# A decoder layer on one core: the residual's factor folded into its addition, an early table load, two banks and one transpose given later ticks

## The chip, the cores and the metric

The kernel runs on one core of one Trainium2 chip. A core has five engines that work side by side, each through its own queue of instructions in program order: TensorE (PE) multiplies matrices out of SBUF into PSUM, VectorE (DVE) and ScalarE (ACT) do elementwise work, GpSimd (POOL) does some too, and SyncE (SP) issues most of the DMA transfers. An instruction that waits holds everything behind it in its own queue. The metric is the time of one execution in microseconds (us) on the device; less is better.

## The reference

One decoder layer on a prompt of 512 tokens and on 8 samples of one token each. What matters here, cut down:

```
x (512 x 1024 prompt rows, 8 x 1024 sample rows), ALPHA = 2 ** 0.25
h   = x * (1 + scale) + shift                    # adaLN from c @ w_ada
att = block-sparse attention, 8 heads of 64      # samples: over a paged K/V cache
mls = matrix memory (mLSTM), 4 heads of 128      # samples: from the states C, n, m
mix = concat(att, mls) @ w_out
x1  = layernorm(ALPHA * x + gate1 * mix)         # first residual
f   = (silu(h2 @ w_gate) * (h2 @ w_up)) @ w_down # h2: x1 modulated
y   = layernorm(ALPHA * x1 + gate2 * f)          # second residual
```

The outputs are y, the new K/V rows and the updated mLSTM states, all fp32.

## The kernel before

Each fp32 matrix is split into a high and a low part (`whi`, `wlo`; `hT_hi`, `hT_lo`; `mixM_hi`, `mixM_lo`; `h_hi`, `h_lo`), and a product is three matmuls. The weights come in 512 KB tiles (`raw`) by DMA, are cast on ACT (`whi`, L240) and subtracted on DVE (`wlo`, L241), and are then used by the main matmuls (L406 in the projections and the FFN's start, L665 in the FFN's body).

The whole program is one list, written in the order of recording. Main matmuls run in groups of six, and after each group a `tick()` lets every side job ("lane") record its next piece, then records the split of one weight tile, then issues loads. `yield n` in a lane means: come back n ticks later. So a lane's `yield` decides between which main groups its instructions stand in each engine's queue. PSUM has 8 banks of 512 columns, handed out in a queue: the bank given back first is taken next, and its new user waits until the last reader of the old contents is done. `put_later` gives a bank back one tick after the recording of that reader, `banks.put` at once:

```
    def put_later(*bs):

        def later():
            banks.put(*bs)
            return
            yield
        spawn(later(), 1)
```

The places that the change touches, in the order of time:

- Samples' attention (L1318 to L1327): the probabilities are transposed on PE into the bank `ps_sp` (L1321, L1322), copied out by DVE (L1325, L1326, written to `vo` by the trace's names), and the bank is given back. Some groups later `ps_pv` (L1339, L1342, L1352) takes the products with the values, DVE masks them (`Z`, L1356), and that bank is given back.
- Samples' mLSTM (L1544 to L1553): ACT scales the heads' rows (L1544), DVE multiplies them by the gate (L1547), PE transposes them (L1551, `ps_h`), and DVE copies the result (`mixsT`, L1553). Around it in time lies the end of the prompt's mLSTM: the keys' scaling (ACT L1196, `mk`), the heads' outputs (ACT L1122, `hm`; PE L1140, `ps_hm`; ACT L1145 and DVE L1146 to `mixM_hi` and `mixM_lo`), and the new states (PE L1205, `ps_C`; ACT L1208).
- `ln1_rows` (L1590 on) loads the prompt's rows x1 and multiplies the four tiles by ALPHA on ACT (L1597), one a tick; then, among other things, it loads the samples' rows `xs` (L1603) and computes the columns of the first norm.
- `residual` (L1636) computes `rtmp = ps * gate` (L1639) and `dst = dst + rtmp` (L1640). The out-projection's `ev_out` calls it eight times, for four row tiles by two halves; the samples' rows and the second residual call it too.
- `ln_rows` (L1618) loads the norm's vectors lg and lb (L1623, L1624) and, 12 ticks after their loads, multiplies them by ALPHA on ACT (L1628).
- The FFN's start, `ffn_first`, with the first Silu at L1821; `ln1_tile` (L1707, L1711, L412) prepares its rows tile by tile.

Of the kernel before, what the change touches and what calls it, by code (L numbers as in the profile page):

```python
# [13 lines left out]
AF = mybir.ActivationFunctionType  # L14
ALU = mybir.AluOpType
AX = mybir.AxisListType.X

P = 128
# [3 lines left out]
NT = 4  # L22
# [8 lines left out]
ALPHA = 2.0 ** 0.25  # L31
# [15 lines left out]
def decoder_layer(  # L47
# [7 lines left out]
    nc = tc.nc  # L55
# [34 lines left out]
    banks = Slots(pp, "b", 8, 512)  # L90
# [18 lines left out]
    TT = nc.vector.tensor_tensor  # L109
    TS = nc.vector.tensor_scalar  # L110
    STT = nc.vector.scalar_tensor_tensor
    VCOPY = nc.vector.tensor_copy
    ACOPY = nc.scalar.copy
    ACT = nc.scalar.activation
    PT_ = nc.gpsimd.tensor_tensor
# [14 lines left out]
    def spawn(gen, delay=0):  # L130
        lanes.append([clock[0] + delay, gen])
# [25 lines left out]
# [8 lines that stand above are left out]
    def lane_bank(name, n=1):  # L165
        while lane_free() < n:
            yield 1
        bs = [banks.get(name) for _ in range(n)]
        return bs[0] if n == 1 else bs
# [1087 lines left out]
    def sample_attention(lag_k, lag_v):  # L1257
# [22 lines left out]
        def fetch(i):  # L1280
            for c in range(4):
                page(sets[i % 2][c], cv, 4 * (i // 4) + c, i % 4)
            asked[i] = clock[0]
# [3 lines left out]
        ps = yield from lane_bank("ps_ss")  # L1287
        for j in range(4):
# [10 lines left out]
           in1=ident[:NB, :NB, None].to_broadcast([NB, NB, 8]), op=ALU.mult)  # L1299
# [19 lines left out]
        ps = yield from lane_bank("ps_sp")  # L1319
# [4 lines left out]
        for j in range(4):  # L1324
            VCOPY(out=PTs[:, j, :, :], in_=ps[:, ts(j, 64)].rearrange("p (b h) -> p b h", h=8))  # L1325
        VCOPY(out=PTo, in_=ps[0:NB, 256:320].rearrange("p (b h) -> p b h", h=8))  # L1326
        banks.put(ps)  # L1327
        yield 2
        for g in range(2):
            bank = yield from lane_bank("ps_pv")  # L1330
            for j in range(4):
                i = 4 * g + j
                while clock[0] < asked[i] + lag_v:
                    yield 1
                for c in range(4):
                    if j == 0:

                        o = 8 * (4 * g + c)
                        mm(bank[32 * c:32 * c + 32, :], lhsT=PTw[:, o:o + 32], rhs=sets[i % 2][c],  # L1339
                           start=True, stop=False, tile_position=(0, 32 * c))  # L1340
                    else:
                        mm(bank[32 * c:32 * c + 8, :], lhsT=PTs[:, j, 4 * g + c, :], rhs=sets[i % 2][c],  # L1342
                           start=False, stop=False, tile_position=(0, 32 * c))
                if i < 6:
                    fetch(i + 2)
                elif i == 6:
                    units.put(vu)
                else:
                    halves.put(vh)
                yield 1  # L1350
            for c in range(4):
                mm(bank[32 * c:32 * c + 8, :], lhsT=PTo[:, 4 * g + c, :], rhs=v8, start=False, stop=True,  # L1352
                   tile_position=(0, 32 * c))
            Zu = yield from slot(rows, "Z", spare=1)
            Z = Zu[:, 0:512]
            TT(out=Z.rearrange("p (h d) -> p h d", d=64), in0=bank.rearrange("p (h d) -> p h d", d=64),  # L1356
               in1=hmask[:, :, None].to_broadcast([P, 8, 64]), op=ALU.mult)
            banks.put(bank)
            yield 1
            pa = yield from lane_bank("ps_za")  # L1360
            for f in range(4):
                mm(pa[:, 4 * f:4 * f + 4], lhsT=Z[:, ts(f, P)], rhs=sel4, start=True, stop=True)
            rows.put(Zu)
            VCOPY(out=mixsT[:, 0:4, 4 * g:4 * g + 4], in_=pa[:, 0:16].rearrange("p (f c) -> p f c", c=4))
            banks.put(pa)
# [38 lines left out]
    junk = cst.tile([P, P], F32, name="junk")  # L1404
# [99 lines left out]
    def sample_mlstm(lag):  # L1504
        while "ob" not in sm:
            yield 1
        for h in range(HM):
            hp = slice(32 * h, 32 * h + 32)
            VCOPY(out=fi[hp], in_=sm["ob"][hp, 1:3, :, h])
        spawn(sample_values())  # L1510
        while not (flags.get("mq_s") and flags.get("mk_s")) or clock[0] < flags["mk_s"] + 3:
            yield 1
        for b in range(NB):
            if b % 4 == 0:
                yield from sample_bc(b // 4)
            spawn(sample_state(b))
            yield lag
        while sm_done[0] < NB or "o_s" not in sm or not flags.get("den8"):
            yield 1
        yield 1  # L1520
        ps = yield from lane_bank("ps_nu")
        for j in range(4):
            nc.tensor.transpose(ps[0:NB, ts(j, P)], num_s[:, :, j], ident)
        u8 = yield from slot(halves, "h8")
        h8 = u8[0:NB, :]
        yield 1
        VCOPY(out=h8.rearrange("b (p j) -> b j p", j=4), in_=ps[0:NB, :].rearrange("b (j p) -> b j p", j=4))
        banks.put(ps)
        s = s8
        bn = cst.tile([NB, HM, 8], F32, name="bn8")  # L1530
        for h in range(HM):
            nc.vector.bn_stats(out=bn[:, h, 0:6], in_=h8[:, ts(h, P)])
        for h in range(HM):
            nc.vector.bn_aggr(out=bn[:, h, 6:8], in_=bn[:, h, 0:6])
        TT(out=s[:, 10, :], in0=s[:, 10, :], in1=bn[:, :, 7], op=ALU.mult)
        rsqrt(s[:, 11, :], s[:, 10, :])
        yield 2
        uo = sm["o_s"]
        o_s = uo[0:NB, :]
        TT(out=s[:, 12, :], in0=s[:, 11, :], in1=s[:, 9, :], op=ALU.mult)  # L1540
        STT(out=s[:, 13, :], in0=bn[:, :, 6], scalar=-1.0, in1=s[:, 12, :], op0=ALU.mult, op1=ALU.mult)
        yield 1
        for h in range(HM):
            ACT(out=h8[:, ts(h, P)], in_=h8[:, ts(h, P)], func=AF.Identity, scale=s[:, 12, h:h + 1],  # L1544
                bias=s[:, 13, h:h + 1])
        yield 1
        TT(out=h8, in0=h8, in1=o_s, op=ALU.mult)  # L1547
        yield 2
        ps = yield from lane_bank("ps_h8")
        for h in range(HM):  # L1550
            nc.tensor.transpose(ps[:, ts(h, 8)], h8[:, ts(h, P)], ident[:NB, :NB])  # L1551
        halves.put(u8, uo)
        VCOPY(out=mixsT[:, 4:8, 0:8], in_=ps[:, 0:32].rearrange("p (h b) -> p h b", b=8))  # L1553
        banks.put(ps)
        flags["mixs_m"] = clock[0]


    big2 = {}
# [30 lines left out]
    x1 = []  # L1589

    def ln1_rows():
        for t in range(NT):
            x1.append(get("x1", [D]))
            dma(out=x1[t], in_=xtok[:, t, :])
        yield 5
        for t in range(NT):
            nc.scalar.mul(out=x1[t], in_=x1[t], mul=ALPHA)  # L1597
            yield 1
        while mixM_done[0] < HM:
            yield 1  # L1600
        xsb = wk.tile([P, 3 * T], F32, name="xs1", tag="PT", bufs=2)[0:NB, 0:D]
        big2["xs"] = xsb
        dma(out=xsb, in_=x_sample.rearrange("b s d -> (b s) d"))  # L1603
        yield 2
        TS(out=xsb, in0=xsb, scalar1=ALPHA, scalar2=None, op0=ALU.mult)
        while not flags.get(("Gs", 0)):
            yield 1
        yield 6
        flags["row8"] = clock[0]
        while not all(flags.get(("ada", j)) for j in (6, 7, 8, 9)):  # L1610
            yield 1
        TT(out=a2, in0=adaT[:, 4], in1=lnT[:, 0:8, None].to_broadcast([P, 8, 9]), op=ALU.mult)
        TT(out=b2, in0=adaT[:, 4], in1=lnT[:, 8:16, None].to_broadcast([P, 8, 9]), op=ALU.mult)
        TT(out=b2, in0=b2, in1=adaT[:, 3], op=ALU.add)
        flags["ab2"] = clock[0]
# [17 lines left out]
        s = wk.tile([P, 16], F32, name="ls", tag="ls", bufs=6)  # L1633
        return s[:n]

    def residual(dst, ps, gate, n, pool_add=False):  # L1636
        u = rows.get("rtmp")
        tmp = u[:n, 0:512]
        TT(out=tmp, in0=ps, in1=gate, op=ALU.mult)  # L1639
        (PT_ if pool_add else TT)(out=dst, in0=dst, in1=tmp, op=ALU.add)  # L1640
        rows.put(u)

    def rows_psum(ps):
# [15 lines left out]
    xs_stats = []  # L1659

    def ev_out(n, t, ps):
        residual(x1[t][:, ts(n, 512)], ps, big2["G1"][n], P)
        if n == 0:
            ln1_stats[t] = stat_tile(P)
            nc.vector.bn_stats(out=ln1_stats[t][:, 0:6], in_=x1[t][:, 0:512])
        else:
            spawn(ln1_tile(t))
            lane = lanes.pop()
            lane[0] = clock[0] + next(lane[1])
            lanes.insert(0, lane)  # L1670
# [345 lines left out]
    for gi, (lo_f, hi_f) in enumerate(FF_GROUPS):  # L2016
# [5 lines left out]
        for n in range(2):  # L2022
            ffn["box", gi, n] = {}
            out = []
# [95 lines left out]
    nc.gpsimd.memset(ffn["fsT"], 0.0)  # L2120
    ffn["sacc"] = get("sacc", [512])
    state["spill"] = 2
    ffn_first(2)
    state["spill"] = 0

# [81 lines left out]
```

## Time and profile before

| | |
|---|---|
| median of 3 runs | 788.74 us (788.0 to 789.09) |
| profiled execution | 785.61 us, of which 783.9 us is the span of the trace |
| mean granted TensorE clock | 0.991 |
| PE / PE weight load | 753.5 us (96%) / 620.1 us (79%) |
| DVE / ACT / POOL | 407.0 (52%) / 276.2 (35%) / 135.6 us (17%) |

The span runs from the first to the last instruction of the profiled execution; the 1.71 us by which its own time is longer lie outside. The median belongs to other executions than the profile. A time in the rows is in us from the start of the span.

### The profile page before, as it was taken

How to read it: one execution, taken by the hardware profiler on the slowest of the kernel's cores; microseconds unless marked ns; L12 is line 12 of the kernel's file. 1: busy time of each engine (PE TensorE's matmuls, PEld its weight loads, DVE VectorE, ACT ScalarE, POOL GpSimd, SP SyncE). 2: the span in 40 equal slices, each digit the busy share in tenths (PEclk: the TensorE clock that was granted, in tenths of full speed). 3: DMA queues.
4: the chain of work that ended last, by engine and by line, in shares of the span. 5: the costliest groups of instructions: out<-in, count | busy, mean ns of one | idle time of the engine just before them, and what ended most of it. 6: DMA issues, size and time to landing. Idle time of an engine off the chain costs nothing.

```text
span 783.9 us, 14706 instructions
## 1 busy us (share of the span) xinstructions
PE 753.5 (96%) x5798; PEld 620.1 (79%) x5798; DVE 407.0 (52%) x851; ACT 276.2 (35%) x560; POOL 135.6 (17%) x163
## 2 busy tenths in 40 slices
PE   8899999999989999799899999999999999999995
PEld 6678667688755668656799977999987799999675
DVE  3442378986346388588653434333332242332687
ACT  2341466554333347536442211223221122322300
POOL 2010235342010021000029413100001130000011
PEclk9999999999999999899999999999999999999999
DMA  9965785664689975746423525323223323223002
GB/s 337 370 225 145 266 263 179 215 204 147 187 248 285 325 244 165 246 152 200 139 59 107 136 84 153 89 84 105 88 77 92 95 81 108 82 81 108 1 31 80
DMA packets 105906, 123.11 MB, mean 157 GB/s; under 512 B 8220, under 2 KB 65696, under 8 KB 105836
## 3 DMA queue, kind: packets, MB, share of 16 engines
q1 hardware_dynamic: 97796, 112.97, 45.2%
q10 hardware_dynamic: 7976, 9.20, 3.5%
q8 instruction: 45, 0.74, 0.4%
q14 instruction: 25, 0.20, 0.1%
q0 software_dynamic: 64, 0.01, 0.0%
HBM read 114.98 MB, written 7.17 MB: 156 GB/s over the span
## 4 chain that ended last, share of the span: by engine, by line
PE 70%; DVE 9%; DMA 5%; ACT 4%; issue 3%; SPq 1%; POOL 1%; ACTq 0%; POOLq 0%; DVEq 0%
PE acc L665 35%; PE acc L406 22%; DMA G<-g_scr 2%; DVE wlo L241 2%; PE ps_dn L428 1%; PE ps_ada L420 1%; PE accl L406 1%; DVE rtmp L1639 1%; DVE x L1640 1%; PE ps_sc L823 1%; PE ps_o L886 1%; PE ps_num L1092 1%; PE ps_ms L1069 1%; PE ps_pt L856 1%; PE ps_pv L1342 1%
## 5 line engine op out<-in xcount | busy, mean ns | idle before, releaser
L241 DVE TENSOR_TENSOR wlo<-raw,whi 128x1024 fp32r<-128x1024 f32 x104 | 137.5, 1330 | 117.4 <-ACT whi L240 111.2
L240 ACT CAST whi<-raw 128x1024 fp32r<-128x1024 f32 x104 | 108.1, 1050 | 151.3 <-PE acc L406 66.6
L665 PE MATMUL acc<-h_hi,whi 128*128 128x256 f32 (+1 forms) x640 | 129.3, 283 | 0.0
L665 PE MATMUL acc<-h_lo,whi 128*128 128x256 f32 (+1 forms) x640 | 128.5, 282 | 0.0
L665 PE MATMUL acc<-h_hi,wlo 128*128 128x256 f32 (+1 forms) x640 | 128.3, 282 | 0.0
L665 PEld LDWEIGHTS acc<-h_hi,whi 128*128 128x128 f32 x640 | 98.8, 188 | 2.7 <-issue 2.5
L665 PEld LDWEIGHTS acc<-h_lo,whi 128*128 128x128 f32 x640 | 99.1, 188 | 0.0
L665 PEld LDWEIGHTS acc<-h_hi,wlo 128*128 128x128 f32 x640 | 99.0, 188 | 0.0
L1244 POOL TENSOR_TENSOR kpage<-kpage,qb 128x512 f32<-128x512 f32 x32 | 42.3, 1345 | 77.0 <-DMA kpage<-in_cache_k_dram 77.0
L1788 DVE TENSOR_TENSOR vf<-acc,vf 128x256 f32<-128x256 f32 x20 | 8.5, 425 | 72.9 <-PE acc L665 72.9
L406 PE MATMUL acc<-whi,f_hi 128*128 128x512 f32 x112 | 45.1, 403 | 0.0
L406 PE MATMUL acc<-wlo,f_hi 128*128 128x512 f32 x112 | 44.2, 395 | 0.0
L406 PE MATMUL acc<-whi,f_lo 128*128 128x512 f32 x112 | 44.0, 393 | 0.0
L406 PE MATMUL acc<-whi,hT_hi 128*128 128x512 f32 x96 | 43.2, 450 | 0.0
L1794 POOL COPY fsT<-vf 128x8 f32<-128x8 f32 x20 | 4.8, 240 | 192.9 <-DVE vf L1789 192.9
L412 ACT CAST f_hi<-vf 128x512 fp32r<-128x512 f32 (+1 forms) x24 | 14.0, 585 | 67.8 <-DVE vf L1789 61.8
L406 PE MATMUL acc<-wlo,hT_hi 128*128 128x512 f32 x96 | 37.8, 394 | 0.0
L406 PE MATMUL acc<-whi,hT_lo 128*128 128x512 f32 x96 | 37.8, 394 | 0.0
L1640 POOL TENSOR_TENSOR x<-x,rtmp 128x512 f32<-128x512 f32 x16 | 25.9, 1642 | 64.9 <-DVE rtmp L1639 64.5
L665 PE MATMUL acc<-hT_hi,whi 128*128 128x256 f32 (+1 forms) x160 | 35.5, 303 | 0.0
L665 PE MATMUL acc<-hT_lo,whi 128*128 128x256 f32 (+1 forms) x160 | 32.2, 282 | 0.0
L665 PE MATMUL acc<-hT_hi,wlo 128*128 128x256 f32 (+1 forms) x160 | 32.2, 282 | 0.0
(403 smaller groups left out, 1405.9 us busy)
## 6 DMA issues: line engine op xcount, KB each, us to landing
raw<-in_w_ada_dram SPq DMA_DIRECT2D x32, 512.0 KB
raw<-in_w_in_dram SPq DMA_DIRECT2D x22, 512.0 KB
raw<-in_w_gate_dram SPq DMA_DIRECT2D x44, 256.0 KB
raw<-in_w_up_dram SPq DMA_DIRECT2D x44, 256.0 KB
raw<-in_w_down_dram SPq DMA_DIRECT2D x22, 512.0 KB
raw_a<-in_ada_first_dram SPq DMA_DIRECT2D x16, 512.0 KB
kpage<-in_cache_k_dram SPq DMA_DIRECT2D x32, 256.0 KB
vpage<-in_cache_v_dram SPq DMA_DIRECT2D x32, 256.0 KB
```

The costliest lines, as they stand in the source:

```text
L240: ACOPY(out=t.hi_t, in_=t.raw)
L241: TT(out=t.lo_t, in0=t.raw, in1=t.hi_t, op=ALU.subtract)
L406: mm(ps, lhsT=a, rhs=b, start=start and i == 0, stop=stop and i == n - 1)
L412: ACOPY(out=dst_hi, in_=v)
L420: mm(ps[32 * c:32 * c + 32, 0:P], lhsT=lhs[:, k0 + kk, :], rhs=raw3[:, kk, ts(c, P)], start=start and kk == 0, stop=stop and kk == nk - 1, ...
L428: mm(ps[32 * c:32 * c + 32, 0:256], lhsT=lhs[:, k0 + kk, :], rhs=raw3[:, kk, ts(n, 256)], start=start, stop=stop, tile_position=(0, 32 * c))
L665: mm(accs[d, hf][:, 0:hi - lo], lhsT=w, rhs=two(xx, k)[:, lo:hi], start=k == 0 and i == 0, stop=k == 7 and i == 2)
L823: mm(bs[e][:, 0:n], lhsT=two(qT, pair)[eh, ts(qt, P)], rhs=two(kT, pair)[eh, 0:n], start=True, stop=True, tile_position=(64 * e, 0))
L856: nc.tensor.transpose(ps[:, ts(kt, P)], pr[:, ts(kt, P)], ident)
L1244: PT_(out=ks[i - 4], in0=ks[i - 4], in1=qb, op=ALU.mult)
L1640: (PT_ if pool_add else TT)(out=dst, in0=dst, in1=tmp, op=ALU.add)
L1788: TT(out=v[:, 0:HALF], in0=a[:, 0:HALF], in1=v[:, 0:HALF], op=ALU.mult)
```

## The change

There are five edits. The banks of `ps_sp` and of the masked products are given back a tick later. The samples' heads are transposed 4 ticks after their gating, not 2. The four ACT multiplications of x1 by ALPHA are gone, with their four ticks, and the first residual multiplies in its addition: `dst * ALPHA + rtmp` in one DVE instruction (`STT`, scalar_tensor_tensor) where it had `dst + rtmp` (`TT`). A Silu of one element stands ahead of `ffn_first`.

```
@@ samples' attention
-        banks.put(ps)
+        put_later(ps)
         yield 2
...
-            banks.put(bank)
+            put_later(bank)
             yield 1
@@ samples' mLSTM
         TT(out=h8, in0=h8, in1=o_s, op=ALU.mult)
-        yield 2
+        yield 4
         ps = yield from lane_bank("ps_h8")
@@ ln1_rows
         yield 5
-        for t in range(NT):
-            nc.scalar.mul(out=x1[t], in_=x1[t], mul=ALPHA)
-            yield 1
         while mixM_done[0] < HM:
             yield 1
@@ residual
-    def residual(dst, ps, gate, n, pool_add=False):
+    def residual(dst, ps, gate, n, pool_add=False, scale=None):
         u = rows.get("rtmp")
         tmp = u[:n, 0:512]
         TT(out=tmp, in0=ps, in1=gate, op=ALU.mult)
-        (PT_ if pool_add else TT)(out=dst, in0=dst, in1=tmp, op=ALU.add)
+        if scale is not None:
+            STT(out=dst, in0=dst, scalar=scale, in1=tmp, op0=ALU.mult, op1=ALU.add)
+        else:
+            (PT_ if pool_add else TT)(out=dst, in0=dst, in1=tmp, op=ALU.add)
         rows.put(u)
@@ ev_out
-        residual(x1[t][:, ts(n, 512)], ps, big2["G1"][n], P)
+        residual(x1[t][:, ts(n, 512)], ps, big2["G1"][n], P, scale=ALPHA)
@@ ahead of the FFN
     state["spill"] = 2
+
+    ACT(out=junk[0:1, 0:1], in_=junk[0:1, 0:1], func=AF.Silu)
     ffn_first(2)
```

The change also moves instructions, since ticks and banks decide the order. On PE, where the samples' probabilities have been transposed, the queue before and then the queue of the change:

```order
908 L1322 MATMUL ps_sp<-ident,Pm 8x64
909 L1069 MATMUL ps_ms<-mqT,mkT 128x128
910 L420 MATMUL ps_ada<-raw,siluT 32x128 x8
911 L406 MATMUL acc<-whi,hT_hi 128x512
912 L406 MATMUL acc<-wlo,hT_hi 128x512
```
```order
908 L1322 MATMUL ps_sp<-ident,Pm 8x64
909 L420 MATMUL ps_ada<-raw,siluT 32x128 x8
910 L406 MATMUL acc<-whi,hT_hi 128x512
911 L406 MATMUL acc<-wlo,hT_hi 128x512
912 L406 MATMUL acc<-whi,hT_lo 128x512
```

The score matmul L1069, which took the bank that `ps_sp` had just left, now stands behind L420 and one group of six L406. In the same way the transpose L605 (`ps_adat`) moves from directly behind L1352 to a place two main groups later.

On PE at the end of the prompt's mLSTM, in the second group of the out-projection that uses `mixM`, before and then of the change:

```order
1167 L406 MATMUL acc<-whi,mixM_lo 128x512
1168 L1551 MATMUL ps_h_4320<-ident,h_4153 128x8 x4
1169 L1205 MATMUL ps_C<-mk,mv_3173 128x128 x2
1170 L1205 MATMUL ps_C<-mk,mv_3174 128x128 x2
1171 L1140 MATMUL ps_hm<-ident,hm 128x128 x4
1172 L406 MATMUL acc<-whi,mixM_hi 128x512
```
```order
1167 L406 MATMUL acc<-whi,mixM_lo 128x512
1168 L1205 MATMUL ps_C<-mk,mv_3173 128x128 x2
1169 L1205 MATMUL ps_C<-mk,mv_3174 128x128 x2
1170 L1140 MATMUL ps_hm<-ident,hm 128x128 x4
1171 L406 MATMUL acc<-whi,mixM_hi 128x512
1172 L406 MATMUL acc<-wlo,mixM_hi 128x512
```

The heads' transpose L1551 is no longer ahead of the state matmuls L1205; in the change it stands at 1179, behind this group of six L406 and a further four L1205.

On ACT, ahead of the FFN, before and then of the change (lg and lb are the norm's vectors, L1647 the samples' rows out of PSUM):

```order
315 L412 CAST h_hi_4580<-v_4705 128x2x128
316 L240 CAST whi<-raw 128x1024 x2
317 L1647 COPY rows_sb<-ps_os 128x256
318 L240 CAST whi<-raw 128x1024 x2
322 L412 CAST h_hi_4580<-vs 128x2x8
323 L240 CAST whi<-raw 128x1024 x2
324 L1821 ACT_TABLE_LOAD
325 L1821 ACTIVATE vf<-acc 128x256
```
```order
308 L412 CAST h_hi_4576<-v_4697 128x2x128
309 L1625 ACTIVATE lg<-lg 128x512 x2
310 L1625 ACTIVATE lb<-lb 128x512 x2
311 L240 CAST whi<-raw 128x1024 x2
312 L1647 COPY rows_sb<-ps_os 128x256
313 L240 CAST whi<-raw 128x1024 x2
317 L412 CAST h_hi_4576<-vs 128x2x8
318 L2124 ACT_TABLE_LOAD
319 L2124 ACTIVATE junk<-junk 1x1
320 L240 CAST whi<-raw 128x1024 x2
```

Of these, the scaling of lg and lb (L1628, now L1625) stood eight casts and four L1711 groups earlier before, between two single L240; the table load stood behind the last two L240 before, and stands ahead of them now.

## Rows read from the trace of the kernel before

**Rows 1.** The page: busy time by engine.

```profile
PE 753.5 (96%) x5798; PEld 620.1 (79%) x5798; DVE 407.0 (52%) x851; ACT 276.2 (35%) x560; POOL 135.6 (17%) x163
```

**Rows 2.** PE's waits: for what, us in total, times, longest.

```profile
PE ps_h L1551 <- ACT x L1597: 4.7, 1, 4.7
...
PE ps_adat L605 <- DVE Z L1356: 0.8, 1, 0.8
```

**Rows 3.** Timeline, 226 to 230: start, duration, [idle before <- releaser].

```profile
228.76 0.46 PE L1069 MATMUL ps_ms<-mqT,mkT 128*128 128x128 f32 x2 [1.49 <-DVE vo L1326]
```

**Rows 4.** Timeline of PE, 316 to 329.

```profile
321.89 0.56 PE L1551 MATMUL ps_h<-ident,h 8*128 8x8 f32 x4 [4.69 <-ACT x L1597]
322.38 2.08 PE L1205 MATMUL ps_C<-mk,mv 128*128 128x128 f32 x8
...
326.39 0.46 PE L406 MATMUL acc<-whi,mixM_hi 128*128 128x512 f32 x1
...
328.86 0.48 PE L406 MATMUL acc<-whi,mixM_hi 128*128 128x512 f32 x1
```

**Rows 5.** Timelines of ACT and of DVE, 316 to 323.

```profile
316.75 1.05 ACT L1597 ACTIVATE x<-x 128x1024 f32<-128x1024 f32 x1
317.71 1.26 ACT L1122 ACTIVATE hm<-hm,s 128x128 f32<-128x128 f32 x4
...
319.81 1.10 ACT L1196 ACTIVATE mk<-ps_mk,gin 128x128 f32<-128x128 f32 x4
...
319.94 1.22 DVE L241 TENSOR_TENSOR wlo<-raw,whi 128x1024 fp32r<-128x1024 f32 x1 [2.37 <-ACT whi L240]
321.08 0.67 DVE L1547 TENSOR_TENSOR h<-h,mo 8x512 f32<-8x512 f32 x1
321.68 0.67 DVE L1571 SCALAR_TENSOR_TENSOR G<-G,bG 128x512 f32<-128x512 f32 x1
```

**Rows 6.** Windows: us; PE, PEld, DVE, ACT, POOL busy; granted clock; DMA share; GB/s.

```profile
28.00:30.00 2.00, 2.00 (x7) 1.57 (x6) 0.18 (x1) 0.16 (x1) 0.00 (x0) 0.61 1.07 396
322.00:326.50 4.50, 4.50 (x20) 4.18 (x21) 2.21 (x4) 1.64 (x3) 0.00 (x0) 0.50 0.90 233
250.00:270.00 20.00, 19.18 (x148) 12.39 (x144) 5.70 (x18) 7.91 (x17) 1.86 (x4) 1.00 1.00 340
330.00:345.00 15.00, 15.00 (x150) 9.51 (x149) 13.07 (x20) 5.04 (x8) 0.55 (x1) 1.00 0.27 86
390.00:396.00 6.00, 3.80 (x25) 3.04 (x25) 2.62 (x7) 4.73 (x16) 0.00 (x0) 1.00 0.38 112
```

**Rows 7.** Timeline of PE, 24 to 27.

```profile
26.25 0.80 PE L406 MATMUL acc<-hT_hi,whi 128*128 128x512 f32 x1 [2.10 <-ACT hT_hi L519]
```

**Rows 8.** Timelines of ACT, DVE and PE, 349 to 367.

```profile
350.48 1.15 ACT L1628 ACTIVATE lg<-lg 128x512 f32<-128x512 f32 x2
351.53 1.13 ACT L1628 ACTIVATE lb<-lb 128x512 f32<-128x512 f32 x2
...
363.57 2.09 ACT L240 CAST whi<-raw 128x1024 fp32r<-128x1024 f32 x2
...
364.74 2.36 DVE L241 TENSOR_TENSOR wlo<-raw,whi 128x1024 fp32r<-128x1024 f32 x2 [0.49 <-ACT whi L240]
...
366.24 0.40 PE L406 MATMUL acc<-wlo,mixM_hi 128*128 128x512 f32 x1
```

**Rows 9.** Timelines of ACT and of PE, 384 to 393.

```profile
384.76 1.28 ACT L1821 ACT_TABLE_LOAD   x1
386.06 0.39 ACT L1821 ACTIVATE vf<-acc 128x256 f32<-128x256 f32 x1
...
385.11 0.39 PE L406 MATMUL acc<-h_hi,wlo 128*128 128x256 f32 x1 [0.40 <-DVE wlo L241]
...
392.87 0.39 PE L406 MATMUL acc<-h_hi,whi 128*128 128x264 f32 x1 [2.06 <-ACT h_hi L412]
```

**Rows 10.** Durations at one line (ns min/median/max): L1640.

```profile
L1640 DVE TENSOR_TENSOR x<-x,rtmp x15: 691/693/695, 331.3 to 773.2; 128x512 f32<-128x512 f32 x15
```

## Prediction

> **What bounds the kernel now.** I read the busy times first: PE is busy for 96% of the span, DVE and ACT for 52% and 35% [rows 1]. So a gain can come only from the few stretches in which PE stands still or runs slowly, and PE's waits name them. The largest of all is 4.7 us, a single one, ahead of L1551; two smaller ones, 1.49 us ahead of L1069 and 0.8 us ahead of L605, also stand beside lines of the change [rows 2, 3]. Then I went to each place in the timeline, and last to the granted clock by windows. [...] The wait at L1551 is credited to ACT's scaling of x1, but L1551 transposes what DVE's L1547 writes, which ends at 321.75; L1547 stood behind a `wlo` that waited 2.37 us for its cast [rows 5], and that cast stood in ACT's queue behind L1597 and L1122. [...]
>
> **Edit 1, `ps_sp` given back later.** L1069 took the bank that `ps_sp` had just left, so it waited for DVE's copies out of it. In the new order L420 and six L406 stand ahead of it, whose operands are there. Its other operand, and the bank that it now gets, were ready before 228.8. The 1.49 us [rows 3] go. What is late next is L1339, the samples' value product, which gets `vo` later in PE's order than it is ready. Bounds 0 and -1.49; I take -1.49, since PE has no other wait in the neighbourhood.
>
> **Edit 2, the masked products' bank.** L605 took the bank that `Z` was still being read from, and waited 0.8 us [rows 2]; two groups of six L406 now stand ahead of it. Bounds 0 and -0.81; I take -0.8.
>
> **Edits 3 and 4 at 317 to 329.** PE's last L406 ends at 321.89 - 4.69 = 317.2 [rows 4]. What stands next now is a group of four state matmuls L1205 (each counted twice in the trace, so x8), not L1551. Three of the four use keys that were scaled long before: 0.7 us of work, to 317.9. The fourth needs the first of four L1196. In ACT's queue one L1597 less stands ahead of these: it took the queue from 316.75 to 317.71, 0.96 us, so they start at 319.81 - 0.96 = 318.85, the first ends at 319.1 and the last at 319.95, at 1.10 us for the four [rows 5]. PE does the fourth matmul at 319.1 and L1140 at 319.95. It stands still for 1.2 us and then 0.6 us, where it stood still for 4.69 us.
>
> How much lies between there and the next main group, which started at 328.86? From 321.89 to 326.39 it was 4.50 us at half clock, so 2.25 at full; from 326.39 to 328.86 it was 2.47 at full: together 4.72 us [rows 4, 6]. Of this the first L1205 group (322.38 to the next instruction, 1.87 us at half clock, so 0.94) is already done. From 319.95 PE needs 4.72 - 0.94 = 3.78 us, and gets to that group at 323.7: **5.1 us earlier**, if the clock stays up. L1551 itself, now 11 instructions later in PE's queue, finds L1547 done: with its cast 0.96 us earlier, that ends near 320.8. The high and low parts that the group at 323.7 needs come from L1140 through an ACT cast and a DVE subtraction, near 323.0; so 0.7 us is the cover here. The ceiling is 4.69 + 2.25 = 6.9 us, with no wait left; the floor, with the clock down for 4.5 us again, is 5.1 - 2.25 = 2.9.
>
> Of the four L1597 only this place counts: the other two ahead of it stood in ACT's slack, and the last was behind L1196.
>
> **What edits 3 and 4 move.** The samples' rows `mixsT` and the norm's flags come at other ticks, and lg and lb are loaded and scaled later. Before, their four scalings (1.15 + 1.13 us, 2.17 from 350.48 to 352.65) lay in an idle stretch of ACT. Now they stand behind the last of four L1711 blocks, which kept ACT busy until 363.57, and directly ahead of the two casts at 363.57 [rows 8]. Both casts go 2.17 us later. DVE was waiting for the first one (0.49 us idle at 364.74), and PE used its `wlo` at 366.24, just 0.3 us after it was there (half of 2.36 behind 364.74) [rows 8]. So PE stands still for 2.17 - 0.3 = 1.9 us here. Behind it the samples' rows go on through DVE, which is 2.0 us late by then. I take **+2.0**; bounds 0 (if PE is held elsewhere just then, so that ACT catches up) and +2.17. The loads of lg and lb now stand in SP's queue behind those of the samples' rows, and cost nothing as long as they land before 363.
>
> **The addition on DVE.** Eight `TT` of 0.693 us [rows 10] become `STT`. The nearest row is L1571, an `STT` of the same 128x512 in fp32, at 0.67 us [rows 5]. So I take 0. [...]
>
> **Edit 5, Silu's table.** The load and one ACTIVATE of one element stand directly behind the samples' casts and ahead of two L240 casts, so no idle time hides them. The load cost 1.28 us at 384.76, between these casts and L1821 [rows 9]; it is moved ahead of the casts, not removed. The extra ACTIVATE is at most the 0.39 us of L1821 (a 128x256), and I take 0.2. The casts then come some 1.5 us later, and PE's wait at 385.11 grows from 0.40 to 1.9. But PE waits again at 392.87, for 2.06 us, on what ACT makes from 386 on [rows 9], and ACT gets there only 0.2 later. The 1.5 us is taken out of that wait. Net **+0.2**, bounds 0 and +1.5 (nothing absorbed).
>
> **The sum**, from the profiled execution's 785.61 us: -1.5 - 0.8 - 5.1 + 2.0 + 0.2 = -5.2, so 780.4. The median is 3.1 above the profiled execution, and I carry the difference over: 788.74 - 5.2 = **783.5 us**. A change within 0.2% (1.6 us) cannot be told from none.
>
> **The rivals.**
>
> *The clock falls at the shortened gap*, too. For: a wait of 2.10 us at 26.25 was followed by a granted clock of 0.61 [rows 6, 7]. Against: the wait of 2.06 us at 392.87 left it at 1.00 [rows 6, 9], and here a matmul lies between 1.2 and 0.6 us. It gives back 2.25: 785.8 us. Chance 0.19.
>
> *The first 2.3 us are eaten.* From 250 to 270 the DMA share is 1.00 at 340 GB/s [rows 6]; if the weights' transfers then set the pace, PE just waits for one later. Against: PE has one wait, of 0.8 us, in those 20 us, and it was no DMA. 785.8 us, chance 0.12; together with the clock, 788.1, chance 0.07.
>
> *The moved scalings cost nothing*, 783.5 - 2.0 = 781.5. For: the table that sets ACT's queue is an order, not a time, and PE's slack before 363 may have grown. Chance 0.09. *Edit 5 is not absorbed*: +1.3, 784.8, chance 0.06.
>
> *The clock falls at every gap of about 2 us*, and the kernel gets slower. The change leaves three: here, the new one at 366, and the one at 385 that grows to 1.9. Each fall costs the 2.25 us that the stretch to 326.5 cost [rows 6]. It decides from the third fall on: 3 x 2.25 = 6.75 is more than 5.2, so 790.3 us. For it speaks 26.25, against it 392.87. [...] The chance of this rival is 0.1.
>
> *The additions are half as fast.* Eight times 0.69 is 5.5 us; from 330 to 345 DVE is busy for 13.07 of 15 us [rows 6], so most would show. 783.5 + 5.5 = 789.0 us. It needs over 0.65 us more for each; no row of the trace has an `STT` of this shape like that. [...] Chance 0.03.
>
> **How the numbers follow.** The forecast has 0.34, and the rivals, in their order, 0.19, 0.12, 0.07, 0.09, 0.06, 0.1 and 0.03. Below 787.2 (faster by over 0.2%) lie the forecast, the fallen clock, the eaten start, the free scalings and the table: 0.8. Within 0.2% lie 788.1, 789.0 and half of the three falls, whose 790.3 stands just at the edge: 0.15. The other half, 0.05, is slower. The range reaches up to the fallen clock with an eaten start and leaves out the two rivals above it, 0.13; below, it takes in the free scalings and a part of the ceiling at 317: 780.8 to 788.2.
>
> **What would show it.** L1069 and L605 without idle time ahead of them. Between 317 and 325 two short waits of L1205 and L1140 on L1196, and a granted clock of 1.00 behind them. A new wait of about 1.9 us for `wlo` in the group that uses `mixM` near 360, with the four L1625 ahead of its cast. The table load ahead of two L240, a longer wait for `wlo` and a shorter one for `h_hi`. `STT` at L1638 near 0.69 us. The prediction is wrong if the clock is at 0.50 behind a gap, or if PE's second wait at the FFN's start does not shrink.

## The result

| | median us | executions |
|---|---|---|
| before | 788.37 (785.42 to 789.09) | 4 |
| changed | 779.22 (776.97 to 780.14) | 4 |

The ratio is 0.9898, with a 95% interval of 0.9871 to 0.9924: faster, by 6 to 10 us (the quotient of the two medians alone is 0.9884). That is more than was forecast, and the time lies below the stated range. Two later sets of twelve executions each, beside executions of the kernel before on the same chip, gave 0.9923 (0.9896 to 0.9950) and 0.9935 (0.9912 to 0.9958), with medians of 781.38 and 780.85 us; the three intervals overlap. The forecast's ratio, 783.5 to 788.74, is 0.9934. Two executions in the sets below, one of the kernel before at 1036.58 us and one of g2_alpha at 1836.65 us, lie far from all others and are left out of the ratios.

The profiled execution of the changed kernel took 779.0 us, with a span of 777.3 us and a mean granted clock of 0.996. PE's waits in it, those that answer to [rows 2] and those that are new:

```profile
PE acc L406 <- DVE wlo L241: 3.3, 4, 1.5
PE acc L406 <- ACT whi L240: 1.6, 2, 0.9
...
PE acc L406 <- DVE adaT L608: 1.2, 1, 1.2
PE acc L406 <- ACT h_hi L412: 0.9, 1, 0.9
...
PE ps_C L1205 <- ACT mk L1196: 0.5, 1, 0.5
```

The waits ahead of L1551, L1069 (on `vo`) and L605 are gone. In their place stand waits for `whi`, for `adaT`, and a short one for `mk`. Where the time went is read from the start of the same PE instruction in the two traces; each difference between two rows of this table is what the stretch between them gave:

| PE instruction | before | changed | earlier by | given in the stretch |
|---|---|---|---|---|
| L1321, ahead of the first instruction that moved | 226.76 | 225.32 | 1.44 | 1.44 |
| L1339 (edit 1 lies before it) | 232.70 | 229.54 | 3.16 | 1.72 |
| last L406 ahead of the heads' transpose (edit 2) | 316.82 | 313.49 | 3.33 | 0.17 |
| first L406 of the next group but one (edits 3, 4) | 328.86 | 320.00 | 8.86 | 5.53 |
| L406 that waits for `wlo` | 349.03 | 340.17 | 8.86 | 0 |
| the FFN start's first wait (lg and lb) | 377.68 | 370.79 | 6.89 | -1.97 |
| its last wait (edit 5) | 392.87 | 386.29 | 6.58 | -0.31 |
| end of the span | 783.9 | 777.3 | 6.6 | 0 |

So the places of the change give 1.72 + 0.17 + 5.53 - 1.97 - 0.31 = 5.14 us in these two profiles, and 1.44 us lie where the two kernels have the same instructions. Two of these figures are to be read beside the other profiles. PE's instructions up to L1321 stand in the same order in all 17 profiles of this document, and L1321 starts between 224.29 and 230.21 us in them; so the 1.44 us can't be put down to the change. And from L1339 to the last L406 ahead of the heads' transpose PE needed 83.4 to 85.3 us, with edit 2 or without, so that its 0.17 can't be told from nothing.

Where L1069 had waited 1.49 us [rows 3], timeline of PE in the changed kernel:

```profile
225.62 0.22 PE L1322 MATMUL ps_sp<-ident,Pm 64*8 64x64 f32 x1
225.77 0.64 PE L420 MATMUL ps_ada<-raw,siluT 128*32 128x128 f32 x16
...
227.84 0.38 PE L1069 MATMUL ps_ms<-mqT,mkT 128*128 128x128 f32 x2
```

L420 follows at once, and L1069 has no idle time ahead of it. Where PE had stood still for 4.69 us [rows 4], timeline of PE:

```profile
313.49 0.39 PE L406 MATMUL acc<-whi,mixM_lo 128*128 128x512 f32 x1
313.72 0.83 PE L1205 MATMUL ps_C<-mk,mv 128*128 128x128 f32 x6
315.03 0.49 PE L1205 MATMUL ps_C<-mk,mv 128*128 128x128 f32 x2 [0.48 <-ACT mk L1196]
315.78 0.66 PE L1140 MATMUL ps_hm<-ident,hm 128*128 128x128 f32 x4 [0.26 <-ACT mk L1196]
...
318.66 0.41 PE L1551 MATMUL ps_h<-ident,h 8*128 8x8 f32 x4
...
320.00 0.48 PE L406 MATMUL acc<-whi,mixM_hi 128*128 128x512 f32 x1
```

Three of the four state matmuls run at once, the fourth and L1140 wait for their keys for 0.48 and 0.26 us, and L1551 waits for nothing. The clock does not fall, by the windows (columns as in [rows 6], where this stretch had 0.50):

```profile
313.00:318.00 5.00, 4.26 (x25) 3.45 (x24) 3.58 (x5) 4.41 (x11) 0.00 (x0) 1.00 0.68 243
318.00:323.00 5.00, 4.99 (x60) 3.96 (x59) 2.36 (x5) 1.83 (x4) 0.00 (x0) 1.00 0.90 266
```

Where ACT now scales lg and lb [rows 8], timelines of ACT and PE:

```profile
354.73 1.24 ACT L1625 ACTIVATE lg<-lg 128x512 f32<-128x512 f32 x2
355.78 1.22 ACT L1625 ACTIVATE lb<-lb 128x512 f32<-128x512 f32 x2
356.82 2.06 ACT L240 CAST whi<-raw 128x1024 fp32r<-128x1024 f32 x2
...
357.99 0.50 PE L406 MATMUL acc<-whi,mixM_hi 128*128 128x512 f32 x1 [0.68 <-ACT whi L240]
...
359.25 0.50 PE L406 MATMUL acc<-wlo,mixM_hi 128*128 128x512 f32 x1 [0.76 <-DVE wlo L241]
```

The casts come right behind the four scalings, and PE waits first for the cast and then for DVE's subtraction: 1.44 us, and the first matmul behind each wait takes 0.50 us, those that follow 0.39 or 0.40. At the FFN's start [rows 9], timelines of ACT and PE:

```profile
375.98 1.28 ACT L2124 ACT_TABLE_LOAD   x1
377.28 0.20 ACT L2124 ACTIVATE junk<-junk 1x1 f32<-1x1 f32 x1
377.39 1.97 ACT L240 CAST whi<-raw 128x1024 fp32r<-128x1024 f32 x2
...
378.46 0.38 PE L406 MATMUL acc<-h_hi,whi 128*128 128x256 f32 x1 [0.88 <-ACT whi L240]
...
379.72 0.39 PE L406 MATMUL acc<-h_hi,wlo 128*128 128x256 f32 x1 [0.76 <-DVE wlo L241]
...
386.29 0.39 PE L406 MATMUL acc<-h_hi,whi 128*128 128x264 f32 x1 [0.87 <-ACT h_hi L412]
```

Table load, casts and PE's waits stand as they were forecast: 0.88 + 0.76 in place of 0.40, and 0.87 in place of 2.06. The additions, by line (ns min/median/max), against 693 of [rows 10]:

```profile
L1638 DVE SCALAR_TENSOR_TENSOR x<-x,rtmp x8: 691/692/694, 322.4 to 371.4; 128x512 f32<-128x512 f32 x8
```

And a wait that the prediction did not have, timelines of DVE and PE:

```profile
293.35 0.18 DVE L608 SCALAR_TENSOR_TENSOR adaT<-ps_adat,cols 128x36 f32<-128x36 f32 x1
...
293.59 0.50 PE L406 MATMUL acc<-whi,mixA_hi 128*128 128x512 f32 x1 [1.18 <-DVE adaT L608]
```

### The profile page after: what moved, and what is told of

The parts are those of the page before. It is cut to its first block, busy times and chain, and to the rows that moved or that the text cites. A ratio compares the mean times of both kernels' runs of the same rounds, so it can differ in the third digit from the quotient of the medians.

```text
span 777.3 us, 14706 instructions
## 1 busy us (share of the span) xinstructions
PE 751.8 (97%) x5798; PEld 618.2 (80%) x5798; DVE 406.8 (52%) x851; ACT 272.5 (35%) x557; POOL 136.6 (18%) x163
## 4 chain that ended last, share of the span: by engine, by line
PE 70%; DVE 9%; DMA 6%; ACT 5%; issue 3%; SPq 1%; POOL 1%; ACTq 0%; POOLq 0%; DVEq 0%
PE acc L665 35%; PE acc L406 22%; DMA G<-g_scr 2%; DVE wlo L241 2%; ACT v L1711 1%; PE ps_dn L428 1%; PE ps_ada L420 1%; PE accl L406 1%; PE ps_ms L1069 1%; PE ps_sc L823 1%; DVE rtmp L1636 1%; PE ps_num L1092 1%; PE ps_o L886 1%; PE ps_pt L856 1%; PE ps_pv L1342 1%
## 5 line engine op out<-in xcount | busy, mean ns | idle before, releaser
L240 ACT CAST whi<-raw 128x1024 fp32r<-128x1024 f32 x104 | 108.1, 1050 | 154.2 <-issue 65.6
L1244 POOL TENSOR_TENSOR kpage<-kpage,qb 128x512 f32<-128x512 f32 x32 | 44.2, 1408 | 73.6 <-DMA kpage<-in_cache_k_dram 73.6
L406 PE MATMUL acc<-whi,f_hi 128*128 128x512 f32 x112 | 45.1, 403 | 0.0
L406 PE MATMUL acc<-wlo,f_hi 128*128 128x512 f32 x112 | 44.2, 395 | 0.0
L406 PE MATMUL acc<-whi,f_lo 128*128 128x512 f32 x112 | 44.0, 393 | 0.0
L406 PE MATMUL acc<-whi,hT_hi 128*128 128x512 f32 x96 | 43.3, 451 | 0.0
L406 PE MATMUL acc<-wlo,hT_hi 128*128 128x512 f32 x96 | 37.8, 394 | 0.0
L406 PE MATMUL acc<-whi,hT_lo 128*128 128x512 f32 x96 | 37.8, 394 | 0.0
L1640 POOL TENSOR_TENSOR x<-x,rtmp 128x512 f32<-128x512 f32 x16 | 25.9, 1643 | 64.9 <-DVE rtmp L1636 64.5
```

Source lines behind the costliest of these rows:

```text
L240: ACOPY(out=t.hi_t, in_=t.raw)
L406: mm(ps, lhsT=a, rhs=b, start=start and i == 0, stop=stop and i == n - 1)
L1244: PT_(out=ks[i - 4], in0=ks[i - 4], in1=qb, op=ALU.mult)
```

## The experiments

Ratios are against executions of the kernel before on the same chip, with 95% intervals; 0.001 is 0.79 us. Two theories stood at the start. A: the change is worth about 5 us, place by place as in the table, and the rest of the 8 is how single executions differ. B: the change is worth 8 us in the usual execution.

| run | what is in it | executions | median us | ratio (95% interval) |
|---|---|---|---|---|
| e1_null | the kernel before | 12 | 785.83 | 0.9997 (0.9977 to 1.0016) |
| e2_banks | edits 1, 2 | 12 | 784.62 | 0.9961 (0.9940 to 0.9982) |
| e3_fold | edits 3, 4 | 12 | 786.77 | 0.9997 (0.9976 to 1.0018) |
| e4_table | edit 5 | 12 | 785.52 | 0.9984 (0.9961 to 1.0006) |
| f1_after | all five | 12 | 781.38 | 0.9923 (0.9896 to 0.9950) |
| f2_ln10 | all, lg and lb scaled earlier | 6 | 777.92 | 0.9889 (0.9867 to 0.9911) |
| f3_ln10_table | as f2, table load in idle time | 6 | 777.61 | 0.9888 (0.9866 to 0.9910) |
| g1_tick4 | edit 3 | 12 | 786.48 | 1.0002 (0.9977 to 1.0026) |
| g2_alpha | edit 4 | 12 | 786.28 | 0.9991 (0.9965 to 1.0016) |
| h1_bank1 | edit 1 | 12 | 784.34 | 0.9965 (0.9943 to 0.9988) |
| h2_best_z0 | as f3, edit 2 for the first group only | 6 | 776.71 | 0.9880 (0.9848 to 0.9912) |
| k1_fold_table | edits 3, 4, 5 | 12 | 784.23 | 0.9967 (0.9943 to 0.9991) |
| k2_after | all five | 12 | 780.85 | 0.9935 (0.9912 to 0.9958) |

### The kernel before against itself

e1_null has no edit. 

> The kernel before, unchanged, as a run of its own. Theory A (the change is worth 5.1 us by place, and the remaining 3 us of the measured 8 come from how single executions of the kernel before differ): the ratio is 1.000 with an interval of some 0.3% either way, and its profile differs from the first one of the kernel before by 1 to 3 us in places ahead of 226 us. Theory B (the change is worth 8 us in the usual execution, since the wait at L1551 and the half clock behind it usually cost more than the first profile shows): the profile shows over 8 us from the last L406 ahead of L1551 to the main group that started at 328.86, where the first had 12.0 with the work in it, and more half clock.

The ratio is 0.9997. Its profile has the same 4.69 us ahead of L1551 as the first one, and the same half clock behind (0.50 from 322 to 326.5), so B's reason for a larger gain isn't there. Its L1321 starts at 226.12 us, 0.64 earlier than in the first profile, less than the 1 to 3 us that A expected. Its twelve executions lie between 785.38 us at a mean granted clock of 0.992 and 789.63 at 0.985, and the slower ones mostly have the lower clock. Where it can fall is seen when the profile of a slower execution is laid beside it. Windows of e1_null, and then of e3_fold, which runs the same instructions up to 300 us:

```profile
131.00:136.00 5.00, 5.00 (x66) 4.63 (x65) 2.75 (x5) 4.02 (x14) 2.59 (x2) 1.00 0.65 207
...
390.00:396.00 6.00, 3.79 (x26) 3.04 (x25) 2.59 (x7) 4.73 (x15) 0.00 (x0) 1.00 0.34 99
```
```profile
131.00:136.00 5.00, 4.89 (x26) 4.80 (x27) 2.46 (x10) 2.40 (x8) 0.77 (x1) 0.66 0.86 276
234.00:238.00 4.00, 4.00 (x14) 3.13 (x12) 0.00 (x0) 1.04 (x1) 0.00 (x0) 0.57 0.81 290
```

In e3_fold PE needed 14.36 us from L823 at 131.11 to L886 at 145.47, where e1_null needed 13.00: some 1.4 us for one such stretch. Ahead of it PE had waited 1.87 us in the one and 1.57 in the other.

### The edits in groups

e2_banks has only the two `put_later`:

```
-        banks.put(ps)
+        put_later(ps)
...
-            banks.put(bank)
+            put_later(bank)
```

> Edits 1 and 2 alone, on the kernel before. Theory A: -1.9 us (-0.24%): the wait at L1069 of 1.5 us and that at L605 of 0.8 gone, a new one near 293 for DVE's adaT of about 1.2 us. Theory B: -2.3 us or more, with no new wait in the profile that lasts.

It gave 3.1 us (1.4 to 4.7); the interval holds what A says and what B says. The new wait is there, 1.18 us at 293.90, and the wait ahead of L1551 is 3.81 us in place of 4.69: the new wait lets ACT catch up, and 0.9 us of it comes back there.

e3_fold is edits 3 and 4 (the addition as in the change):

```
-        yield 2
+        yield 4
...
-        for t in range(NT):
-            nc.scalar.mul(out=x1[t], in_=x1[t], mul=ALPHA)
-            yield 1
```

> Edits 3 and 4 alone, on the kernel before. Theory A: -3.5 us (-0.45%): the stretch at L1551 shorter by 5.5, a new wait for wlo in the out-projection's last third of 1.4 to 2.0. Theory B: -6 us or more.

Its times show nothing, 0.9997 (-1.9 to +1.4 us), though its profile has the short waits (1.38 and 0.26 us) where 4.69 stood, a clock of 1.00 from 320 to 327, and 0.67 + 0.76 us of new waits near 367. From L605 to the wait at 349 it needed 89.20 us, where the kernel before needed 94.58: 5.4 us less, as A says. So the place gains, and the times as a whole don't show it. The same kernel was profiled twice more:

> Edits 3 and 4 once more, one execution, to see where low clock lies. Theory A: from L605 to the wait at 349 the time is 5.4 us less than before, whatever the total; half clock ahead of 300 us varies from execution to execution, and is not more than in executions of the kernel before. Theory C: a stretch of half clock that the kernel before does not have, each time.

> As the look before: a third execution of edits 3 and 4, for where half clock lies.

They took 783.2 and 785.8 us, with 4.4 and 4.8 us less from L605 to the wait at 349 (90.19 and 89.75). Half clock lay behind 390 in the one, and behind 26, 229 and 392 in the other. Windows of the first:

```profile
26.00:30.00 4.00, 3.58 (x14) 2.71 (x15) 1.93 (x6) 0.98 (x3) 0.00 (x0) 1.00 1.04 399
316.00:323.00 7.00, 5.35 (x38) 4.49 (x38) 4.67 (x7) 4.69 (x12) 0.00 (x0) 1.00 0.77 258
390.00:394.00 4.00, 4.00 (x22) 4.00 (x21) 2.02 (x5) 3.14 (x7) 0.00 (x0) 0.57 0.00 0
```

Its wait at 389.00 is 2.08 us, that of e1_null at 392.67 is 2.06, and only the first has half clock behind it.

e4_table is edit 5:

```
+    ACT(out=junk[0:1, 0:1], in_=junk[0:1, 0:1], func=AF.Silu)
     ffn_first(2)
```

> Edit 5 alone, on the kernel before. Theory A: +0.3 us, not to be told from nothing: PE's wait for wlo at the FFN's start grows by 1.2 and the next one for h_hi shrinks by as much. Rival: the early load takes a table load off the first Silu and gives 1 us.

1.3 us less, not to be told from nothing (-3.1 to +0.5). The profile has the forecast's waits, 0.89 for the cast and 0.76 for `wlo`, and no wait of 2 us behind them, but half clock from 388 to 391 (0.88 in the mean from 386 to 400). No load is saved: the traces of the kernel before and of the changed kernel have five table loads each, all of 1.28 us, and Silu's is the last, at 384.76 and at 375.98.

### The parts of edits 3 and 4

g1_tick4 is edit 3 alone (the first two lines of e3's diff), g2_alpha edit 4 alone (the others).

> Edit 3 alone (the heads' transposes two ticks later, the four L1597 still there). Theory A (by place): PE's wait ahead of L1551 goes, and the fourth L1205 waits for its key until about 320.1, so 2.2 us of standing still and 0.6 at L1140 in place of 4.69; the main group of 328.86 starts 4.2 us earlier if the clock stays at 1.00, 2 us if it falls. No cost at 366, since the four ticks and lg's scaling stay: -2 to -4 us (-0.25 to -0.5%). Theory C (what the stretch at L1551 gives is lost again to lower clock behind other gaps in the same execution): the clock averages no more than in the kernel before and the time is the same.

> Edit 4 alone (no L1597, the factor in the residual's addition). Theory A: L1551 still stands ahead of L1205, its wait is 3.7 us in place of 4.69 and the half clock behind it stays; at 366 the wait for wlo comes up with 1.4 to 2.0 us: +0.5 to +1 us (slower, not to be told from nothing). The STT at the line of the addition takes 0.69 us like the TT. If it took twice as long, DVE would be 5 us longer busy. Theory C: the same within noise.

Neither moved the time (1.0002 and 0.9991), and the expectation was wrong on where the waits near 366 come from. They are edit 3's. PE's idle rows of g1_tick4 there and at the heads:

```profile
322.33 0.49 PE L1205 MATMUL ps_C<-mk,mv 128*128 128x128 f32 x2 [2.34 <-ACT mk L1196]
...
365.28 0.50 PE L406 MATMUL acc<-whi,mixM_hi 128*128 128x512 f32 x1 [0.66 <-ACT whi L240]
...
366.54 0.50 PE L406 MATMUL acc<-wlo,mixM_hi 128*128 128x512 f32 x1 [0.76 <-DVE wlo L241]
```

In g2_alpha there is no wait between 349 and 377, and at the heads only one us was won:

```profile
321.56 0.56 PE L1551 MATMUL ps_h<-ident,h 8*128 8x8 f32 x4 [3.73 <-ACT whi L240]
```

The flag of the samples' heads is set two ticks later by edit 3, so lg and lb are scaled two ticks later, and that is behind the L1711 blocks. Edit 4, with four ticks fewer, does not bring that. Edit 4 alone keeps a wait of 3.7 us and the half clock; edit 3 alone keeps the clock up behind its 2.34 us (main matmuls of 0.39 or 0.40 us from the second on, where g2_alpha has 0.63), but pays 2.0 us at 366. From the last L406 ahead of the heads to the wait at 349, the six profiles without edit 3 needed 31.6 to 32.7 us, the kernel before 32.21 and g2_alpha 31.63 among them; g1_tick4 needed 28.53 (3.7 less than the kernel before, where 4.2 was expected), and e3_fold, with both edits, 27.56. So most of the gain at this place is edit 3's, and edit 4 adds 1.0 us once edit 3 is there.

### The bank edits

h1_bank1 is the first `put_later`, on `ps`. 

> Edit 1 alone. Theory A: -1.5 us (-0.2%): the wait at L1069 near 228 gone, nothing new; and half clock no longer comes behind that place (e4's profile had it there), which would add up to -1.5 more on average.

2.8 us less (0.9 to 4.5): more than the 1.49 us, as the expectation left room for. The profiles show why. From L1321 to L1339 PE needed 4.22 us in each of the eight profiles that have edit 1, and 5.94 to 8.73 us, 7.24 in the mean, in the nine that haven't. The first profile of the kernel before, from which the prediction was read, has the 5.94: the smallest of the nine, as is its wait of 1.49 us. The longest is that of k1_fold_table, timeline of PE:

```profile
228.32 0.51 PE L1069 MATMUL ps_ms<-mqT,mkT 128*128 128x128 f32 x2 [2.76 <-DVE vo L1326]
```

So by these profiles edit 1 is worth 3.0 us in the mean. The two banks together (3.1 us by the times) are not seen to be worth more than the first alone.

### The changed kernel again, and what it leaves

f1_after and k2_after are the changed kernel. 

> The changed kernel once more, to be compared with the kernel before on another chip. Theory A: between -5 and -6.5 us (-0.65 to -0.8%) when both are run often. Theory B: -8 us (-1.0%) again.

> The changed kernel a third time, with executions of the kernel before on the same chip. If its first four executions were lucky ones: a ratio near 0.993 (-5 to -6 us) as in the second set. If not: 0.990.

-6.1 and -5.1 us, by their ratios: A. B's 8 us did not come again; the first interval (-8.2 to -3.9) just reaches it, the second (-6.9 to -3.3) doesn't.

f2_ln10 takes two ticks off the delay of lg and lb:

```
         if scale != 1.0:
-            yield 12
+            yield 10
```

> The changed kernel, with lg and lb scaled two ticks earlier, so that the four ACT instructions stand between two casts again and not behind the L1711 blocks. If the 2.0 us at 358 to 360 are theirs: the waits of 0.68 and 0.76 us for whi and wlo go, and the kernel is 1.5 to 2.0 us faster than the changed one. Rival (the waits are set by the casts' slots or by the L1711 blocks themselves): the waits stay and the time is that of the changed kernel.

777.92 against f1's 781.38 on the same chip, and both waits are gone. From the wait at 349 to the FFN's first wait it needed 28.64 us, f1 30.61, so 1.97 us are theirs, as expected; the medians differ by more (3.5 us, with intervals that overlap). The scalings stand in idle time again, timeline of ACT:

```profile
341.98 1.15 ACT L1625 ACTIVATE lg<-lg 128x512 f32<-128x512 f32 x2
343.03 1.14 ACT L1625 ACTIVATE lb<-lb 128x512 f32<-128x512 f32 x2
345.05 1.04 ACT L240 CAST whi<-raw 128x1024 fp32r<-128x1024 f32 x1 [0.88 <-PE acc L406]
```

f3_ln10_table records the one-element Silu with the samples' norm too:

```
                 TS(out=xs, in0=xs, ...)
+                ACT(out=junk[0:1, 0:1], in_=junk[0:1, 0:1], func=AF.Silu)
                 yield 2
```

> As the run before, and the one-element Silu recorded with the samples' norm, ahead of ACT's last cast before its idle 11 us, so that the table load lies in idle time. Expected: the two waits at the FFN's start, 0.88 and 0.76 us, go back to 0.4 or less; the later wait for h_hi is set by the chain of L1711 and L412, which starts 1.3 us earlier if L1821 does, so 0.5 to 1.3 us faster than the run before. Rival (L1821 is held by PE's accumulator, not by ACT): nothing gained.

The load lies in idle time. At the FFN's start PE waits 0.40 us where the changed kernel had 0.88 and 0.76, and later 0.94 us for `h_hi` where that had 0.87; timelines of ACT and PE:

```profile
357.66 1.28 ACT L1754 ACT_TABLE_LOAD   x1
...
360.54 1.05 ACT L240 CAST whi<-raw 128x1024 fp32r<-128x1024 f32 x1 [1.39 <-PE acc L406]
...
375.47 0.39 PE L406 MATMUL acc<-h_hi,wlo 128*128 128x256 f32 x1 [0.40 <-DVE wlo L241]
...
382.11 0.39 PE L406 MATMUL acc<-h_hi,whi 128*128 128x264 f32 x1 [0.94 <-ACT h_hi L412]
```

From its first wait at 368.04 to the last at 382.11 it needed 14.07 us, the changed kernel 15.50. The time (777.61) can't be told from f2's.

h2_best_z0 gives the second group's bank back at once, as before:

```
-            put_later(bank)
+            (put_later if g == 0 else banks.put)(bank)
```

> The changed kernel with lg and lb scaled earlier, the table load in idle time, and edit 2 for the first group of samples only, so that the order near 290 is that of the kernel before. If the new wait of 1.18 us for DVE's adaT near 293 comes from edit 2's second bank: it goes, and the kernel is 0.5 to 1.2 us faster than e-f3 (777.6), -1.2 to -1.35% against the kernel before. Rival (DVE is the limit there whatever the order): the wait moves to another line and the time stays.

The wait for `adaT` is gone, so it is the second bank's. But 0.9 us of it comes up at the next place, where the changed kernel had 0.48:

```profile
315.60 0.49 PE L1205 MATMUL ps_C<-mk,mv 128*128 128x128 f32 x2 [1.38 <-ACT mk L1196]
```

Of the 1.18 us 0.3 would be left, less than the expectation's 0.5, and by place not even that is seen: from L605 to the wait at 349 h2 needed 86.16 us and f3 86.12. The medians (776.71 and 777.61) don't tell the two kernels apart either. By their medians, of six executions each, f2, f3 and h2 are some 3 us or more faster than the changed kernel's 781; from L1321 to the end of the span their profiles needed 2.2 to 4.0 us less than its three.

### Edits 3, 4 and 5

k1_fold_table is e3's diff and e4's together.

> Edits 3, 4 and 5 without the bank edits. In the looks at edits 3 and 4 the wait of 2.06 us near 390 was followed by half clock in two of three executions, which it was not in the kernel before. Edit 5 splits that wait into shorter ones. Theory D (the gain at L1551 was lost to half clock behind that wait, and edit 5 gives it back): -3 to -4 us (-0.4 to -0.5%), more than edits 3 and 4 (0.0%) and edit 5 (-0.16%) apart. Rival (the parts just add up): -0.2%.

-2.6 us (-0.7 to -4.5), between the two, with intervals that overlap both. Its profile has half clock behind 228, where PE waited 2.76 us, and behind 385, where it waited 0.86 and 0.76 (granted clock 0.50 from 229 to 232 and from 386 to 389). So splitting the wait does not keep the clock up for certain, and by the times this theory is neither shown nor refuted. By place something speaks for it: from the FFN's first wait to the end of the span e4, f2 and k1, with half clock behind the split waits, needed 406.2 to 406.6 us, no more than profiles without half clock there (406.2 to 407.0), while g1, g3, g4 and h1, with half clock behind the whole wait of 2.06 us, needed 407.1 to 407.7.

## Why the prediction was right and wrong

**Edit 1: right in its cause, and too small.** It gave 1.72 us in the pair of profiles where 1.5 was forecast, but 3.0 in the mean of all profiles and 2.8 in the times. The term was read from a single profile, which happened to have the shortest of nine waits (1.49 to 2.76 us). Of the nine profiles that have the wait, five also have half clock behind it (e3, e4, g1, g4, k1; 7.64 to 8.73 us from L1321 to L1339) and four have not (the kernel before, e1, g2, g3; 5.94 to 6.65); of the eight without the wait none has it there.

**Edit 2: the term of -0.8 was mis-sized; it measured -0.17, within what the profiles scatter.** The wait at L605 went. The step that failed is "two groups of six L406 now stand ahead of it" as the whole price: the second group's bank, given back later, moves L1069 and the adaT copy near 290, and PE waits there for 1.18 us. h2_best_z0 shows that this bank is the cause. Up to 0.9 us of this wait is given back at L1205 (0.48 us where h2 waits 1.38).

**Edits 3 and 4 at 317: right.** 5.53 for 5.1, with two short waits on L1196 and the clock at 1.00. Of the 5.53 us 0.9 are what PE had waited for `adaT` before; without that wait, in e3_fold, the stretch gives 4.65, with waits of 1.38 and 0.26 us where 1.2 and 0.6 were forecast. The half clock did not come at the shortened gap in any of the eleven profiles that have edit 3, also not behind g1's 2.34 us; that rival had 0.19.

**What edits 3 and 4 move: right in size, 1.97 for 2.0, and too wide in its cause.** It is edit 3 alone (g1, g2), and f2_ln10 shows that it can be had back.

**The addition: right.** 692 ns in place of 693. That an addition might take twice as long, as the rival with the 5.5 us had it, is shown by no run: the eight `STT` took 691 to 694 ns each in the changed kernel.

**Edit 5: right.** 0.31 for 0.2, absorbed where the prediction said.

**What was wrong is the last step of the sum: "the median is 3.1 above the profiled execution, and I carry the difference over".** The places of the change gave 5.14 us in the pair of profiles, for a forecast of 5.2. That they agree so closely is partly luck: over all profiles edit 1 gives 3.0 us in the mean, edit 2 nothing, and from the last L406 ahead of the heads to the end of the span the three profiles of the changed kernel needed 463.8 us, the six without edit 3 467.2 in the mean, 3.4 less; together 6.4. The 3.1 us were taken as something that every execution has, and 788.74, the median of three executions, as the base. In the five later sets, of 17 to 35 executions each, the kernel before has medians of 786.3 to 787.2, and its executions, but for the one at 1036.58, lie between 782.6 and 793.7; from 786.4, the base of f1 and k2, the forecast of -5.2 gives 781.2, and they measured 781.4 and 780.85. So 2.3 us of the miss of 4.3 were the base, and the remaining 2 go with four executions of the changed kernel that had a mean clock of 0.995, where the sets of twelve have 0.993; these four were not compared place by place. On which chip the first set ran is not on record. A slower or faster chip alone would not explain it, since its base was higher than in the later sets and its changed kernel lower. The range came from the terms of the change alone. It should have held what two medians of a few executions can do when single ones of one set differ by 7 to 10 us.

The rivals: the three falls did not come, nor the half-speed addition; the moved scalings were not free (1.97 us), and edit 5 was absorbed but for 0.31. The first 2.3 us were not eaten by the transfers: the stretch behind edit 1 kept its 1.72, and what edit 2 lost went to `adaT`, not to a DMA.

**What stays open.** Counted from L605, e3_fold, g3 and g4 win 4.4 to 5.4 us up to 349 and g1_tick4 2.5 (92.08 us), all lose 2.0 behind it, and the times show nothing won. Counted from the last L406 ahead of the heads to the end of the span, less is left to look for: e3, g3 and g4 needed 465.1 to 465.9 us, g1 466.3, the six profiles without edit 3 466.9 to 467.9. That is some 1.7 and 1.0 us in the mean, and the intervals of the times of e3 (-1.9 to +1.4) and g1 (-1.8 to +2.0) hold it. Part of what is lost is half clock elsewhere. The wait of 2.06 to 2.08 us near 390 had half clock behind it in g1, g3, g4 and h1 (granted clock 0.88 in the mean from 386 to 400), and not in the kernel before, e1, e2, e3 and g2 (1.00). That taking half clock away at 322 brings it at 390 is not shown: e3 has it at neither place and h1 at both. What decides whether the clock falls behind a wait of about 2 us stays open.

## What to carry to other kernels

Look at what stands directly ahead in each in-order queue, not at the instruction that a wait is credited to: L1597 was named, but the transpose's place in PE's queue was the larger part. Moving it gave 3.7 us at this place, and taking L1597 away alone left a wait of 3.73 us. When a tick moves a flag, list everything that waits for the flag: here two ticks put four scalings from idle time in front of a cast that PE needed, 2 us that one number gave back. A wait read from one profile is one draw: that at L1069 lay between 1.49 and 2.76 us in nine. And before a range is stated for a change of under one per cent, look at how far single executions of the kernel before lie apart, and at their clock: three executions are no base for it.

## What the runs showed of the hardware

A wait of about the same length at the same place is followed by the lower level of the clock (granted clock 0.50) in some executions and not in others. The wait near 26 had half clock behind it in the kernel before and in the first profile of the changed kernel (2.10 and 2.07 us; granted clock 0.57 and 0.58 from 26 to 30), and not in k2 (2.23 us; 1.00). A longer wait can leave the clock up where a shorter one doesn't: at L1069, near 228, 1.80 us in g4 were followed by main matmuls of 0.63 us, the length that they have in k1 at a granted clock of 0.50, and 2.20 us in g3 by main matmuls of 0.39 or 0.40 from the second on. Two short waits in a row can do it as well: the 0.86 and 0.76 us at 384 in k1, with half clock from 385 to 389 (0.50 from 386 on), and the 0.89 and 0.76 us in e4 (0.88 in the mean from 386 to 400), but not the 0.88 and 0.76 us in the first profile of the changed kernel and in k2 (1.00 behind them). One stretch of half clock, at 131 in e3 (granted clock 0.66 from 131 to 136), cost some 1.4 us, and the profile of f3_ln10_table, whose granted clock averages 0.997, is the fastest execution of all, 774.81 us. The waits at L1551 were followed by half clock in the profiles of the kernel before and of e1_null (4.69 us; granted clock 0.50 from 322 to 326.5) and in those of h1 and g2 (4.68 and 3.73 us; main matmuls of 0.63 us). Waits of about 2 us were followed by it only in some profiles.
